# Queueing the negation of each prefetched projection tile behind an evacuation on ScalarE, in a hybrid decoder block

## The chip, the cores and the metric

The kernel runs on one core of one Trainium2 chip. The metric is the device time of one execution in microseconds (us), as the median over several runs. The engines that matter are TensorE (PE: matmuls into PSUM), VectorE (DVE), ScalarE (ACT), GpSimd (POOL) and SyncE (SP). Each engine works through its own instruction list in the order in which the program was laid out; semaphores tie the lists together. DMAs are issued from SP's list and from POOL's.

## The reference, cut to what matters

One decoder layer over a sequence of 512 tokens and a width of 1024, in float32: an RMS norm, one wide input projection `proj = h @ w_in`, cut into the parts `xr, gr, q, k, v, iq, ik, iw, g_a, g_b`; a recurrent branch (a causal convolution of `xr`, an RG-LRU scan, times `gelu(gr)`); a sparse attention branch, in which an indexer (`iq, ik, iw`) picks 128 keys for each query; then

```
merged = sigmoid(g_a) * y_a + sigmoid(g_b) * y_b
x = x + rms_norm(merged @ w_o)
x = x + rms_norm((silu(h @ w_ffn_gate) * (h @ w_ffn_up)) @ w_ffn_down)
```

The part at issue is `h @ w_in`.

## The kernel before

**Splitting.** Float32 precision is kept by splitting each operand into a rounded part `hi` and a rest `lo = x - hi`. One projection of 128 output columns (`mm3_steps`, L278) is then 24 matmuls of 128x512: for each of eight row blocks `hi*hi` (L281), `hi*lo` (L283), `lo*hi` (L285), all into one PSUM bank from `acc()` (L66), of which there are two that take turns.

**Units.** The weight tiles are numbered as *units* in the order in which they are used: u0 to u3 the indexer's queries, u4 to u11 the eight `gr` tiles, u12 to u27 pairs of `xr` tiles and pairs of `g_a` tiles in turn, u28 one `g_b` tile, u29 the first keys tile, u30 and u31 the first two queries tiles, u32 to u39 the RNN's output weights, u40 to u53 the other queries, keys and `g_b` tiles. Those of `w_in` except u0 and u1 are of kind "d" (44 of them): `do_load` (L204) issues a DMA on POOL (L220) that lands the tile rounded as `hi`. `do_split` (L240) then does two things: ACT writes `lo = -hi` (L243, the *negation*), and POOL issues a second DMA of the same tile that adds it to `lo` (L244, the *adding DMA*). The tiles live in six places: four named `ws`, and two pairs named `raw`. Every third unit uses a `raw` pair. A place is free again when PE is through with its unit.

**The order.** `take(u)` (L258) is called just before the matmuls of unit u. It loads up to u+5 and splits up to u+3. After the matmuls an ACT instruction evacuates the bank: `rope` (L474) for queries and keys, the gelu (L569) for `gr`, a copy into `xpad` (L577) for `xr`, a copy into `ma` (L626) for `g_a`, a copy into `gs` (L681) for `g_b`. A scheduler lays out each engine's list beforehand, by a simulated timeline: it may put a negation earlier on ACT than the program text does, when the simulation finds its data there and ACT free. On the chip an engine doesn't step past an instruction that waits.

**Around it.** In the gelu stage (about 60 to 127 us) PE also does the indexer's score matmuls; `lru_inputs` (L571) runs from `xpad` over `xc` (three DVE steps, L581) and its split `xcs` (L84) to the gate matmuls (L587, L588) and the sigmoids, and `lru_scan` (L600) goes on with exponentials, square roots and a scan. From u40 on the projections are threaded between the steps of attention, where PE's order is that of the program.

Of the kernel before, what the change touches and what calls it, by code (L numbers as in the profile page):

```python
# [11 lines left out]
AF = mybir.ActivationFunctionType  # L12
# [4 lines left out]
S = 512  # L17
# [28 lines left out]
def hybrid_block(ctx: ExitStack, tc: tile.TileContext, x, norm_mix_pre, w_in, conv_w, conv_b, rg_w_a,  # L46
# [4 lines left out]
    V, SC, G, PE = nc.vector, nc.scalar, nc.gpsimd, nc.tensor  # L51
# [14 lines left out]
    def acc():  # L66
        return psum.tile([P, 512], F32, name="acc", tag="acc")

    def ps_s():
        return ps_mix.tile([P, 512], F32, name="ps_s", tag="s", bufs=3)  # L70

    def ps_t():
        return ps_mix.tile([P, 512], F32, name="ps_t", tag="t", bufs=2)
# [4 lines left out]
    def f(ap):  # L78
        return ap.bitcast(F32)

    after = {}

    def split(src, hi, lo, lo_engine=None):
        return SC.copy(hi, src).ins, (lo_engine or V).tensor_tensor(lo, src, f(hi), op=A.subtract).ins  # L84
# [33 lines left out]
    def heap(shape, dt=F32R, name="hp"):  # L118
        return mixp.tile(shape, dt, name=name, tag="heap", bufs=14)
# [22 lines left out]
    for c in range(2):  # L142
        ps = ps_t()
# [96 lines left out]
    def do_split(u):  # L240
        if units[u][3] == "d":
            hi, lo = held.pop(u)
            SC.mul(lo, f(hi), -1.0)  # L243
            G.dma_start(lo, units[u][1], accum_op=A.add)  # L244
            wss[u] = [h.rearrange("p (k c) -> p k c", c=P) for h in (hi, lo)]
            return
        raw, ws = held.pop(u)
        with ExitStack() as order:
            for ins in after.pop(u + 2, ()) if u < 2 else ():
                order.enter_context(tc.issue_after(ins))  # L250
            split(raw, ws[:, 0], ws[:, 1])
        wss[u] = ws[:, 0], ws[:, 1]
# [5 lines left out]
    def take(u, ahead=3):  # L258
        load_ahead(u)
        while state["split"] <= min(u + ahead, state["load"] - 1):  # L260
            s = state["split"]
            if units[s][3] == "r" or s > u + 2 and units[s][3] == "s":
                break
            do_split(s)
            state["split"] += 1
        return wss.pop(u)
# [11 lines left out]
    def mm3_steps(ps, ws, hi, lo, order=None):  # L278
        order = order or list(range(KT))
        for n, k in enumerate(order):  # L280
            pe(PE.matmul(ps, ws[0][:, k, :], hi(k), start=(n == 0), stop=False))  # L281
            yield
            pe(PE.matmul(ps, ws[0][:, k, :], lo(k), start=False, stop=False))  # L283
            yield
            pe(PE.matmul(ps, ws[1][:, k, :], hi(k), start=False, stop=(n == len(order) - 1)))  # L285
            yield

    def mm3(*args, **kw):
        for _ in mm3_steps(*args, **kw):
            pass  # L290
# [88 lines left out]
    for t in range(NT):  # L379
        if t + 1 < NT:  # L380
            first_norm(t + 1)
        ps = acc()
        for k in range(KT):
            hi, lo = hT[:, 0, k, t * P:(t + 1) * P], hT[:, 1, k, t * P:(t + 1) * P]
# [48 lines left out]
    ps = ps_s()  # L433
# [3 lines left out]
    def col(n, m):  # L437
        return pcol[:, n * KT + m:n * KT + m + 1]
# [28 lines left out]
    ma = [map_.tile([P, S], F32, name=f"ma{m}") for m in range(KT)]  # L467
# [3 lines left out]
    def rope(ps, factor=1.0):  # L471
        xe = tmpp.tile([P, S], F32, name="rp_x", tag="t0")
        xs = tmpp.tile([P, S], F32, name="rp_s", tag="t1")
        SC.activation(xe, ps, AF.Copy, scale=factor)  # L474
        V.stream_shuffle(xs, xe, swap)
        G.tensor_tensor(xe, xe, rope_c, op=A.mult)
        G.tensor_tensor(xs, xs, rope_s, op=A.mult)
        V.tensor_tensor(xe, xe, xs, op=A.add)
        return xe
# [11 lines left out]
    for m in range(4):  # L491
        ps = acc()
        mm3(ps, take(u_iq[m]), h_hi, h_lo)
        iq.append(stack_q(rope(ps)))
# [53 lines left out]
    def load_gate_weights(m):  # L548
        raw = rnnp.tile([P, 2, P], F32, name="gw_raw", tag="gw_raw", bufs=2)
        ws = rnnp.tile([P, 2, 2, P], F32R, name="gw", tag="gw", bufs=2)  # L550
        G.memset(raw, 0.0)
        for n, w in enumerate((rg_w_a, rg_w_x)):
            ld(raw[0:HD, n, 0:HD], w[0, 2 * m])
            ld(raw[HD:P, n, HD:P], w[0, 2 * m + 1])
        split(raw, ws[:, 0], ws[:, 1], G)
        gw[m] = ws

    def shared(shape, tag, bufs):
        return rnnp.tile(shape, F32, name=tag, tag=tag, bufs=bufs)

    ys, gl, rr, tt, iu = [], {}, {}, {}, {}
    last = {}

    def gelu_gate(m):
        ps = acc()
        mm3(ps, take(u_gr[m]), h_hi, h_lo)
        if m % 2 == 0:
            gl[m] = heap([P, 2, S], F32, "gl")
        SC.activation(gl[m - m % 2][:, m % 2, :], ps, AF.Gelu_apprx_tanh)  # L569

    def lru_inputs(m):  # L571
        load_gate_weights(m)
        ps = acc()
        mm3(ps, take(u_xr[m]), h_hi, h_lo)
        xp = tmpp.tile([P, S + 3], F32, name="xpad", tag="t0")
        G.memset(xp[:, 0:3], 0.0)
        SC.copy(xp[:, 3:S + 3], ps)  # L577
        xc = tmpp.tile([P, S], F32, name="xc", tag="t1")
        SC.activation(xc, xp[:, 0:S], AF.Identity, bias=col(4, m), scale=col(0, m))
        for j in range(1, 4):  # L580
            V.scalar_tensor_tensor(xc, xp[:, j:j + S], col(j, m), xc, op0=A.mult, op1=A.add)  # L581
        xs = heap([P, 2, S], name="xcs")
        split(xc, xs[:, 0, :], xs[:, 1, :])
        gps = []
        for n in range(2):
            ps = ps_s()
            PE.matmul(ps, gw[m][:, 0, n, :], xs[:, 0, :], start=True, stop=False)  # L587
            PE.matmul(ps, gw[m][:, 0, n, :], xs[:, 1, :], start=False, stop=False)  # L588
            PE.matmul(ps, gw[m][:, 1, n, :], xs[:, 0, :], start=False, stop=True)
            gps.append(ps)  # L590
        rr[m], tt[m], iu[m] = shared([P, S], "rr", 4), shared([P, S], "tt", 4), shared([P, S], "iu", 4)
        SC.activation(rr[m], gps[0], AF.Sigmoid, bias=col(5, m))
        sig = SC.activation(iu[m], gps[1], AF.Sigmoid, bias=col(6, m))
        with tc.issue_after(sig.ins):
            last[m] = SC.activation(tt[m], rr[m], AF.Tanh, scale=sp4[:, m:m + 1])
        G.tensor_tensor(iu[m], iu[m], xc, op=A.mult)
# [26 lines left out]
    def gate_a(m):  # L623
        ps = acc()
        mm3(ps, take(u_ga[m]), h_hi, h_lo)
        SC.copy(ma[m], ps)  # L626

    for m in range(KT):
        gelu_gate(m)
        drain(3)  # L630
    for m in range(0, KT, 2):
        lru_inputs(m)
        lru_inputs(m + 1)
        if m > 0:
            lru_scan((m - 2, m - 1))
        gate_a(m)
        gate_a(m + 1)
        drain(2)
# [15 lines left out]
    def keys(m):  # L654
        ps = acc()
        yield from mm3_steps(ps, take(u_k[m]), h_hi, h_lo)
        r = rope(ps)
        for n in range(2):
            t = heap([P, 2, S], name="kst")
            src = r[n * HD:(n + 1) * HD]  # L660
            own = t[n * HD:(n + 1) * HD, 0, :]
            oth = t[(1 - n) * HD:(2 - n) * HD, 0, :]
            SC.copy(own, src)
            SC.copy(oth, src)
            V.tensor_tensor(t[0:HD, 1, :], src, f(own), op=A.subtract)
            V.tensor_tensor(t[HD:P, 1, :], src, f(own), op=A.subtract)
            ks[2 * m + n] = t


    def queries(m):  # L670
        ps = acc()
        yield from mm3_steps(ps, take(u_q[m]), h_hi, h_lo)
        qs[m] = stack_q(rope(ps, -(HD ** -0.5)))
# [3 lines left out]
    def gate_b(m):  # L677
        ps = acc()
        yield from mm3_steps(ps, take(u_gb[m]), h_hi, h_lo)
        gs = tmpp.tile([P, S], F32, name="gs", tag="t0")  # L680
        SC.copy(gs, ps)  # L681
        ld(gb_dram[m], gs)

    qs = {}
    for gen in [gate_b(m) for m in range(1)] + [keys(0), queries(0), queries(1)]:
        for _ in gen:
            pass
# [103 lines left out]
    for m in range(KT):  # L791
        ps = acc()
# [38 lines left out]
    def bank2():  # L831
        return psx.tile([P, 512], F32, name="bank2", tag="y", bufs=2)

    ps0 = [bank4() for _ in range(NT)]
    for n, k in enumerate(korder):
        if k % 2 == 0:
            ws = take(u_wo[0, k])
        for t in range(NT):
            hi, lo = mg[k][:, 0, t * P:(t + 1) * P], mg[k][:, 1, t * P:(t + 1) * P]
# [26 lines left out]
    for t in range(NT):  # L866
        ps1 = acc()
        for n, k in enumerate(korder):
            w = wo1[k]
            hi, lo = mg[k][:, 0, t * P:(t + 1) * P], mg[k][:, 1, t * P:(t + 1) * P]  # L870
# [16 lines left out]
        for half in range(2):  # L887
            ps = bank2()
# [286 lines left out]
```

## Time and profile before

| what | value |
|---|---|
| median of 3 runs | 927.35 us (925.54 to 927.96) |
| the profiled execution | 927.87 us, of which its span is 926.1 us |
| ACT busy | 497.4 us (54%) |
| DVE busy | 615.6 us (66%) |
| POOL busy | 229.3 us (25%) |
| mean granted clock of PE | 0.975 |
| TensorE clock in 40 slices, tenths | 9998998999989979999999998999999999999999 |

The times come from executions without the profiler; the rows come from the one profiled execution, and differences are made against its own time. Busy shares say how much an engine did, not what it waited for. A 9 in the row of the clock is full speed, 2.4 GHz; lower digits are slices in which the engine had half of that for a while.

### The profile page before, as it was taken

How to read it: one execution, taken by the hardware profiler on the slowest of the kernel's cores; microseconds unless marked ns; L12 is line 12 of the kernel's file. 1: busy time of each engine (PE TensorE's matmuls, PEld its weight loads, DVE VectorE, ACT ScalarE, POOL GpSimd, SP SyncE). 2: the span in 40 equal slices, each digit the busy share in tenths (PEclk: the TensorE clock that was granted, in tenths of full speed). 3: DMA queues.
4: the chain of work that ended last, by engine and by line, in shares of the span. 5: the costliest groups of instructions: out<-in, count | busy, mean ns of one | idle time of the engine just before them, and what ended most of it. 6: DMA issues, size and time to landing. Idle time of an engine off the chain costs nothing.

```text
span 926.1 us, 12988 instructions
## 1 busy us (share of the span) xinstructions
PE 873.5 (94%) x4811; PEld 750.6 (81%) x4811; DVE 615.6 (66%) x1109; ACT 497.4 (54%) x839; POOL 229.3 (25%) x242
## 2 busy tenths in 40 slices
PE   8989978989979979999999998999999999999996
PEld 5877756767668768888878887999999999988885
DVE  7675667885684148767756558978888887534415
ACT  6344336668733178777754346666666656333302
POOL 3362213355251143221012300323332332100000
PEclk9998998999989979999999999999999999999999
DMA  9667556657534654640454754687887788433203
GB/s 297 136 142 165 113 132 140 142 128 151 145 91 94 156 114 91 119 103 20 124 159 139 234 157 141 155 173 175 186 185 174 185 183 187 154 114 92 69 0 137
DMA packets 65698, 129.74 MB, mean 140 GB/s; under 512 B 8865, under 2 KB 32481, under 8 KB 65634
## 3 DMA queue, kind: packets, MB, share of 16 engines
q0 software_dynamic: 18432, 61.87, 33.3%
q1 hardware_dynamic: 46048, 64.92, 22.4%
q10 hardware_dynamic: 1154, 2.10, 0.6%
q8 instruction: 38, 0.62, 0.3%
q14 instruction: 26, 0.21, 0.1%
HBM read 122.59 MB, written 6.29 MB: 139 GB/s over the span
## 4 chain that ended last, share of the span: by engine, by line
PE 53%; issue 15%; DMA 14%; DVE 7%; ACT 5%; POOL 4%; SPq 0%; POOLq 0%; DVEq 0%; ACTq 0%
DMA ws<-in_t_ff_dram 6%; DMA ws<-in_t_in_dram 4%; PE acc L283 4%; PE acc L281 4%; PE acc L285 4%; PE bank L987 4%; PE bank L985 4%; PE bank L986 4%; PE bank L1060 3%; PE bank L1059 3%; PE bank L1061 3%; PE ps_o L739 2%; PE ps_t L729 2%; PE acc L1060 1%; PE acc L1059 1%
## 5 line engine op out<-in xcount | busy, mean ns | idle before, releaser
L281 PE MATMUL acc<-hT,ws 128*128 128x512 f32 x248 | 101.6, 410 | 8.9 <-ACT xpad L577 5.7
L84 DVE TENSOR_TENSOR ws<-raw,ws 128x1024 fp32r<-128x1024 f32 x44 | 61.2, 1394 | 66.0 <-ACT ws L84 65.8
L283 PE MATMUL acc<-hT,ws 128*128 128x512 f32 x248 | 100.8, 406 | 0.0
L285 PE MATMUL acc<-hT,ws 128*128 128x512 f32 x248 | 100.3, 404 | 0.0
L84 ACT CAST ws<-raw 128x1024 fp32r<-128x1024 f32 x44 | 46.1, 1052 | 70.6 <-PE bank L1061 37.6
L243 ACT ACTIVATE ws<-ws 128x1024 fp32r<-128x1024 f32 x29 | 30.7, 1059 | 88.0 <-DMA ws<-in_t_in_dram 83.0
L979 POOL DMA_DIRECT2D ws<-in_t_ff_dram x40 | 35.3, 883 | 153.7 <-ACT ws L978 80.9
L84 ACT CAST ws<-sums 128x1024 fp32r<-128x1024 f32 x40 | 40.1, 1048 | 50.9 <-DVE sums L969 50.0
L281 PEld LDWEIGHTS acc<-hT,ws 128*128 128x128 f32 x248 | 48.0, 194 | 21.3 <-ACT xpad L577 7.0
L987 PE MATMUL bank<-T,ws 128*128 128x256 f32 x200 | 57.6, 289 | 1.4 <-DMA ws<-in_t_ff_dram 0.8
L985 PE MATMUL bank<-T,ws 128*128 128x256 f32 x200 | 56.5, 283 | 0.4 <-ACT ws L84 0.4
L986 PE MATMUL bank<-T,ws 128*128 128x256 f32 x200 | 56.5, 282 | 0.0
L986 PE MATMUL bank<-B,ws 128*128 128x256 f32 x200 | 56.3, 282 | 0.0
L283 PEld LDWEIGHTS acc<-hT,ws 128*128 128x128 f32 x248 | 48.1, 194 | 10.1
L285 PEld LDWEIGHTS acc<-hT,ws 128*128 128x128 f32 x248 | 47.9, 193 | 10.2
L985 PE MATMUL bank<-B,ws 128*128 128x256 f32 x200 | 56.1, 281 | 0.0
L987 PE MATMUL bank<-B,ws 128*128 128x256 f32 x200 | 55.9, 280 | 0.0
L244 POOL DMA_DIRECT2D ws<-in_t_in_dram x29 | 25.7, 887 | 116.5 <-ACT ws L243 100.0
L281 PE MATMUL acc<-hT,raw 128*128 128x512 f32 x120 | 49.8, 415 | 4.0 <-ACT gl L569 4.0
L84 DVE TENSOR_TENSOR ws<-sums,ws 128x1024 fp32r<-128x1024 f32 x40 | 47.8, 1233 | 7.6 <-ACT ws L84 7.5
L283 PE MATMUL acc<-hT,raw 128*128 128x512 f32 x120 | 50.1, 417 | 0.0
L285 PE MATMUL acc<-hT,raw 128*128 128x512 f32 x120 | 49.6, 413 | 0.0
(330 smaller groups left out, 2716.1 us busy)
## 6 DMA issues: line engine op xcount, KB each, us to landing
ws<-in_t_in_dram POOLq DMA_DIRECT2D x58, 512.0 KB, 5.7
raw<-in_t_ff_dram SPq DMA_DIRECT2D x40, 512.0 KB, 4.5
raw<-in_t_in_dram POOLq DMA_DIRECT2D x30, 512.0 KB, 5.5
raw<-in_w_ffn_down_dram SPq DMA_DIRECT2D x22, 512.0 KB, 3.6
ws<-in_t_ff_dram POOLq DMA_DIRECT2D x20, 512.0 KB, 5.6
ws<-in_t_ff_dram POOLq DMA_DIRECT2D x20, 256.0 KB, 6.8
raw<-in_w_rnn_out_dram SPq DMA_DIRECT2D x8, 512.0 KB, 5.7
raw<-in_w_att_out_dram SPq DMA_DIRECT2D x8, 512.0 KB, 3.7
```

The costliest lines, as they stand in the source:

```text
L84: return SC.copy(hi, src).ins, (lo_engine or V).tensor_tensor(lo, src, f(hi), op=A.subtract).ins
L243: SC.mul(lo, f(hi), -1.0)
L281: pe(PE.matmul(ps, ws[0][:, k, :], hi(k), start=(n == 0), stop=False))
L283: pe(PE.matmul(ps, ws[0][:, k, :], lo(k), start=False, stop=False))
L285: pe(PE.matmul(ps, ws[1][:, k, :], hi(k), start=False, stop=(n == len(order) - 1)))
L979: G.dma_start(dst[:, 1], t_ff[n, m].rearrange("p (k c) -> p k c", c=P)[:, k], accum_op=A.add)
L985: PE.matmul(ps, a[:, 0, k, :], b[:, 0, k, :], start=(k == 0), stop=False)
L986: PE.matmul(ps, a[:, 0, k, :], b[:, 1, k, :], start=False, stop=False)
L987: PE.matmul(ps, a[:, 1, k, :], b[:, 0, k, :], start=False, stop=(k == 3))
L1059: PE.matmul(ps, a[:, 0, ts], b[:, 0, cs], start=(k == 0), stop=False)
L1060: PE.matmul(ps, a[:, 0, ts], b[:, 1, cs], start=False, stop=False)
L1061: PE.matmul(ps, a[:, 1, ts], b[:, 0, cs], start=False, stop=(k == FT - 1))
```

## The change

The negation's place on ACT gets a lower bound. Each of the five evacuations leaves its instruction in `after["evac"]`, and `do_split` lays the negation behind the last one left there, with an order on ACT's own list (`issue_after`). `take(u)` splits unit u+3 before the matmuls of u are laid out, so the last evacuation known is that of u-1: the negation of unit s now stands behind the evacuation of unit s-4. Units u2 and u3 are split before any evacuation is known and are as before. The RNN's output projections (u32 to u39) leave nothing in `after["evac"]`, so the negations of u40 to u43, split while they run or at the start of u40, stand behind that of u31 only.

```diff
     def do_split(u):
         if units[u][3] == "d":
             hi, lo = held.pop(u)
-            SC.mul(lo, f(hi), -1.0)
+            with ExitStack() as order:
+                if "evac" in after:
+                    order.enter_context(tc.issue_after(after["evac"]))
+                SC.mul(lo, f(hi), -1.0)
             G.dma_start(lo, units[u][1], accum_op=A.add)
...
     def rope(ps, factor=1.0):
-        SC.activation(xe, ps, AF.Copy, scale=factor)
+        after["evac"] = SC.activation(xe, ps, AF.Copy, scale=factor).ins
...
     def gelu_gate(m):
-        SC.activation(gl[m - m % 2][:, m % 2, :], ps, AF.Gelu_apprx_tanh)
+        after["evac"] = SC.activation(gl[m - m % 2][:, m % 2, :], ps, AF.Gelu_apprx_tanh).ins
...
     def lru_inputs(m):
-        SC.copy(xp[:, 3:S + 3], ps)
+        after["evac"] = SC.copy(xp[:, 3:S + 3], ps).ins
...
     def gate_a(m):
-        SC.copy(ma[m], ps)
+        after["evac"] = SC.copy(ma[m], ps).ins
...
     def gate_b(m):
-        SC.copy(gs, ps)
+        after["evac"] = SC.copy(gs, ps).ins
```

## Rows read from the trace of the kernel before

**Rows 1.** The page's busy time of each engine: us, share of span, instructions.
```profile
PE 873.5 (94%) x4811; PEld 750.6 (81%) x4811; DVE 615.6 (66%) x1109; ACT 497.4 (54%) x839; POOL 229.3 (25%) x242
```
**Rows 2.** Who waited for whom: us in total, times, longest us.
```profile
POOL ws L244 <- ACT ws L243: 100.0, 23, 7.7
ACT ws L243 <- DMA ws<-in_t_in_dram: 83.0, 23, 7.8
...
ACT raw L243 <- DMA raw<-in_t_in_dram: 26.1, 9, 6.3
...
POOL iu L614 <- ACT tt L611: 15.7, 4, 5.0
```
**Rows 3.** The same view for PE alone.
```profile
PE ps_s L587 <- ACT xcs L84: 6.5, 4, 3.8
PE acc L281 <- ACT xpad L577: 5.7, 3, 2.9
PE ps_t L729 <- DVE pt L84: 5.4, 4, 3.0
...
PE acc L281 <- ACT gl L569: 4.0, 1, 4.0
...
PE acc L281 <- ACT ma L626: 3.0, 1, 3.0
```
**Rows 4.** ACT in time, 128 to 139 us: start, us, instruction, [idle before <- releaser].
```profile
128.50 1.06 ACT L243 ACTIVATE ws<-ws 128x1024 fp32r<-128x1024 f32 x1 [4.98 <-DMA ws<-in_t_in_dram]
129.47 0.57 ACT L577 COPY xpad<-acc 128x512 f32<-128x512 f32 x1
...
137.20 1.06 ACT L243 ACTIVATE raw<-raw 128x1024 fp32r<-128x1024 f32 x1 [6.26 <-DMA raw<-in_t_in_dram]
138.16 0.60 ACT L84 CAST xcs<-xc 128x512 fp32r<-128x512 f32 x1
```
**Rows 5.** ACT in time, three places elsewhere.
```profile
154.22 1.06 ACT L243 ACTIVATE ws<-ws 128x1024 fp32r<-128x1024 f32 x1 [2.57 <-DMA ws<-in_t_in_dram]
...
190.35 1.06 ACT L243 ACTIVATE ws<-ws 128x1024 fp32r<-128x1024 f32 x1 [2.70 <-DMA ws<-in_t_in_dram]
...
335.39 1.06 ACT L243 ACTIVATE ws<-ws 128x1024 fp32r<-128x1024 f32 x1 [5.09 <-issue]
```
**Rows 6.** ACT in time, 58 to 71 us.
```profile
58.89 1.06 ACT L243 ACTIVATE ws<-ws 128x1024 fp32r<-128x1024 f32 x1 [3.89 <-DMA ws<-in_t_in_dram]
...
60.15 0.59 ACT L474 ACTIVATE rp_x<-acc 128x512 f32<-128x512 f32 x1
...
70.61 0.60 ACT L569 ACTIVATE gl<-acc 128x512 f32<-128x512 f32 x1
```
**Rows 7.** PE in stretches of 8 us: busy time (instructions), granted clock, DMA share, GB/s.
```profile
71.26:79.26 8.00, 8.00 (x24) 0.63 0.74 191
...
138.82:146.82 8.00, 7.27 (x24) 0.80 0.61 131
159.90:167.90 8.00, 8.00 (x23) 0.63 0.44 118
196.65:204.65 8.00, 8.00 (x28) 0.79 0.32 81
```
**Rows 8.** PE in time: the first matmuls of units u0 and u1.
```profile
31.19 0.40 PE L281 MATMUL acc<-hT,ws 128*128 128x512 f32 x1
...
36.77 0.39 PE L281 MATMUL acc<-hT,ws 128*128 128x512 f32 x1
```
**Rows 9.** The view of line L244, its last line: from issue to landing.
```profile
DMA to landing us min/median/max: 5.4/5.6/8.8
```
**Rows 10.** POOL in time, 95 to 97 us.
```profile
95.71 0.87 POOL L244 DMA_DIRECT2D ws<-in_t_in_dram  x1 [6.84 <-ACT ws L243]
96.28 0.86 POOL L220 DMA_DIRECT2D ws<-in_t_in_dram  x1
```
**Rows 11.** ACT in time, the negation that waited for the load of rows 10.
```profile
103.36 1.06 ACT L243 ACTIVATE ws<-ws 128x1024 fp32r<-128x1024 f32 x1 [5.85 <-DMA ws<-in_t_in_dram]
```

## The prediction, written before the changed kernel ran

> **What bounds the kernel now.** I read the page first: PE is busy 873.5 us of 926.1, so at most 52.6 us of the span are PE's idle time, and every other engine is far from full [rows 1]. What can be won is PE idle time, and the slow clock that follows it. The list of all waits shows something odd on ACT: the largest waits of this half-idle engine are those of the negation for the DMA of its own tile, 83.0 us in 23 waits and 26.1 us in 9 more, and POOL sits 100.0 us behind the same negations [rows 2]. ACT does nothing else in those 109.1 us, because its list is worked in order. Whether that matters is read from PE's own waits: its long ones end with ACT's evacuations and casts, which shared a list with those negations: `xpad` 5.7 us, `xcs` 6.5, `gl` 4.0, `ma` 3.0; and one of 3.0 that ends with DVE's part of `pt`, itself behind ACT's cast [rows 3].
>
> ACT in time shows the mechanism. At 128.50 a negation starts after 4.98 us of waiting for its DMA, and `xpad`, the evacuation that PE's next projection needs, follows at 129.47; at 137.20 the next one starts after 6.26 us, and `xcs`, for which the gate matmuls wait, follows at 138.16 [rows 4]. Counting negations in unit order (every third goes to a `raw` place), the first is u17's and the second u18's, while `xpad` here is the evacuation of u12. So the list has the negation five units ahead of the evacuation that it holds up, and its tile isn't needed before PE has worked off five projections.
>
> **The change, part by part.** It adds and removes no instruction and no DMA; an order within one engine's list needs no wait of its own. So the direct cost is nil; 44 negations of 1.06 us [rows 4] stay 46.6 us on ACT, at other places.
>
> *What moves.* Unit s's negation goes behind the evacuation of s-4: u17's behind that of u13, that is past `xpad` of u12; u18's, behind u14's, past `xcs`. The same holds at the negations of 154.22 (u20, ahead of the `ma` copy), 190.35 (u25, ahead of an `xpad`), 335.39 (u46, ahead of a `pt` cast) [rows 5] and 58.89 (u8, ahead of the rope evacuation of u3 at 60.15, from which the query stacking runs that the gelu evacuation of 70.61 stood behind) [rows 6]. Not moved are u2, u3, and u40 to u43, so PE's wait for a softmax tile near 322 us, behind u43's negation, stays.
>
> *The stalls that go.* A stall goes if the negation's wait and its 1.06 us exceed it. Near 130 and 138 they do, 4.98 and 6.26 against an `xpad` wait below 2.9 and an `xcs` wait of 3.8 [rows 3, 4]. At 154.22 and 190.35 it is 2.57 + 1.06 = 3.63 and 2.70 + 1.06 = 3.76 against 3.0 (`ma`) and 2.9 (`xpad`): enough by under 1 us. At 335.39 it is 5.09 + 1.06 against 3.0, but a DVE step stands between. At 58.89 it is 3.89 + 1.06 = 4.95 against 4.0, through a chain over POOL and DVE [rows 3, 5, 6].
>
> *The clock.* After a stall PE runs for some us at the lower of its two levels, 1.2 instead of 2.4 GHz: in the 8 us from 71.26, the end of the `gl` stall, the mean granted clock is 0.63, so 0.37 x 8 = 2.96 us are lost; the same after `ma` at 159.90, and (a third such stretch, not shown) after 337.46. After `xcs` at 138.82 it is 0.20 x 8 = 1.60, after `xpad` at 196.65 0.21 x 8 = 1.68 [rows 7].
>
> *The sum.* Two groups:
> - Sure in mechanism: `xpad` 5.7 - 2.9 = 2.8, `xcs` 6.5, its clock 1.6: 10.9 us, in full.
> - Thin margin or a chain through another engine: `xpad` 2.9 + 1.68, `gl` 4.0 + 2.96, `ma` 3.0 + 2.96, `pt` 3.0 + 2.96: 23.5 us, of which I take half, 11.7.
>
> That is 22.6 us; all of it would be 34.4.
>
> *What is late next.* Three things may take some back. First the adding DMA, now issued later: behind the waiting negation on ACT are casts and sigmoids, and behind the adding DMA, on POOL, the loads of later tiles, the rope products and the scan's products; who waits for those is PE, by way of DVE. There are two banks, so PE can't start unit s-2 before the evacuation of s-4, and from there to the start of s lie two projections, 2 x (36.77 - 31.19) = 11.2 us [rows 8]. Negation (1.06) and landing (5.6 median, 8.8 at most) take 6.7 to 9.9 us [rows 4, 9]: it fits, with 1.3 to 4.5 us to spare. Second the load: POOL issues it when PE has freed its place, six units back, and the negation comes after the evacuation two units later, 11.2 us on, against 7.08 us that a load took from its issue at 96.28 to the negation at 103.36 [rows 10, 11]; so that wait mostly ends, and only a new neighbour on ACT pays 1.06 us. Third the recomputed lists: every engine's order shifts a little. For a stall that the trace before doesn't show I can give only bounds: nothing, or the case below. I take one of the size of the second `xpad` stall, 2.9 + 1.68 = 4.6 us.
>
> So 22.6 - 4.6 = 18.0 us come off the profiled execution's 927.87, giving 909.9. That execution lies 0.5 us above the median of 927.35, so the prediction is 909.4, rounded to **909 us**.
>
> One rule speaks against the change. The Trainium skill, "DMA: Bandwidth & Descriptors", section "Queues, rings and completion order", says that each DMA engine takes the descriptors of a ring in ring order. By it, an adding DMA issued right behind a load lands later than one with the ring to itself; the trace agrees, for the load right behind an adding DMA took up to 7.08 us where adding DMAs take 5.6 in the median [rows 9 to 11]. With the load ahead, by this rule, the spare time would be 11.2 - 1.06 - 7.08 = 3.1 us rather than 4.5: enough still, but it is part of the slow rival.
>
> **The rivals.**
> - *All of it* (0.12): no new stall, 927.9 - 34.4 - 0.5 = 893. For it: the negations' 109.1 us [rows 2] are more than three times what is asked of them. Against: some of it hangs on margins below 1 us.
> - *Only the first places* (0.17): the `ma`, later `xpad`, `gl` and `pt` stalls are kept by the table loads, the DVE steps and the casts around them, and only 10.9 us come, less 4.6: 927.9 - 6.3 - 0.5 = 921. For it: those margins.
> - *The wait only changes its name* (0.10): PE's stalls come back under other releasers, or the scheduler puts other waiting work ahead of the evacuations: 927. This is also the case in which the change doesn't do what it says. Against: ACT's busy time is 54% [rows 1], and the loads get 11.2 us.
> - *The adding DMA comes too late* (0.18), slower. Place: the recurrent stage, u16 to u31. A negation held by a neighbour on ACT, or an adding DMA held on POOL behind a scan product (longest wait 5.0 us [rows 2]) and behind a load, takes 1.06 + 7.08 + 5.0 = 13.1 us against 11.2 [rows 8, 10, 11], and PE stops at its third matmul. Priced at 4.6 us a stall as above, four late tiles of the 16 eat the 18.0; at seven, 7 x 4.6 - 18.0 = 14.2 come on top: 941. Against: it takes two delays at once, and a late PE gives the DMA more time.
>
> **How the numbers follow.** The forecast has 0.43, the rivals 0.12, 0.17, 0.10 and 0.18. A difference counts from 0.3%, 2.8 us: faster is below 924.6, slower above 930.1. The forecast and the first two rivals are faster: 0.72; same 0.10; slower 0.18. The range goes from 892 to 931: it leaves out nearly all of the slow rival, and little below.
>
> **What would show it.** Right: in the list of waits the negation's wait for its DMA falls from 109.1 us below 30; ACT in time shows evacuations starting within 1 us of the last matmul in the gelu stage; PE's waits for `xpad`, `xcs`, `gl` and `ma` shrink from 19.2 us (the four rows) to below 8, and the clock's low slices between 60 and 210 us go. POOL's wait for the negation need not fall, since the negation itself is later. Wrong: PE waiting at L285 for a DMA of `ws` or `raw` (the late adding DMA), or the same stalls with table loads or DVE as releasers. Two numbers would break the reasoning: negations that still wait long for loads, or stalls that go without the time going with them.

## The result, and the profile after

The changed kernel takes 890.57 us (median of 4, 889.10 to 891.81) beside 927.38 for the kernel before on the same chip: ratio 0.9606, 95% interval 0.9586 to 0.9626. It is faster by 36.8 us, twice the 18.0 that I forecast. The profiled execution took 890.67 us with a span of 888.8, against 927.87 and 926.1 before.

The page, busy time and the slices of PE's granted clock:

```profile
PE 857.5 (96%) x4811; PEld 740.9 (83%) x4811; DVE 620.6 (70%) x1109; ACT 494.7 (56%) x838; POOL 229.2 (26%) x242
...
PEclk9999999999899999999999999999999999999998
```

PE's busy time fell from 873.5 [rows 1] to 857.5: the same 4811 instructions took 16.0 us less, and the mean granted clock rose from 0.975 to 0.991. PE's idle time (span less busy) fell from 52.6 to 31.3, 21.3 us. The two make up the 37.3 us of the span. The clock's stretches of [rows 7] no longer have their dips; the same windows of the changed kernel (it is elsewhere in its work by then) show PE at the higher of its two levels, 2.4 GHz, throughout (two of the four):

```profile
71.26:79.26 8.00, 8.00 (x38) 1.00 0.99 214
138.82:146.82 8.00, 8.00 (x36) 1.00 0.91 170
```

All waits, the lines that answer to [rows 2]:

```profile
POOL ws L220 <- PE acc L288: 64.4, 14, 11.8
...
POOL ws L247 <- ACT ws L246: 41.8, 14, 7.7
ACT ws L246 <- DMA ws<-in_t_in_dram: 23.2, 3, 8.8
...
POOL raw L247 <- ACT raw L246: 18.4, 7, 6.0
```

The negation's wait for its own DMA fell from 109.1 us in 32 waits to 23.2 in 3, and those three are u40, u42 and u43. The line on top is the one to notice: POOL now issues loads (L220) as soon as **PE** has freed a place, and not as soon as ACT has let it past an adding DMA. PE's own waits, which answer to [rows 3]:

```profile
PE acc L284 <- ACT rp_x L477: 4.1, 1, 4.1
PE ps_t L732 <- DVE pt L84: 2.4, 4, 1.0
...
PE acc L284 <- ACT xpad L580: 1.4, 1, 1.4
...
PE acc L284 <- ACT gl L572: 1.2, 1, 1.2
...
PE ps_t L732 <- ACT sm L717: 0.8, 1, 0.8
```

`xpad`, `gl`, `xcs` (0.2) and `ma` (none) were 19.2 us and are 2.8. Only `rp_x`, u30's rope evacuation behind the casts of the keys, is still near its old size (5.2 before). ACT in the gelu stage:

```profile
93.97 0.60 ACT L572 ACTIVATE gl<-acc 128x512 f32<-128x512 f32 x1 [3.46 <-PE acc L288]
94.47 1.05 ACT L246 ACTIVATE ws<-ws 128x1024 fp32r<-128x1024 f32 x1
...
100.84 0.60 ACT L572 ACTIVATE gl<-acc 128x512 f32<-128x512 f32 x1 [3.60 <-PE acc L288]
101.33 1.05 ACT L246 ACTIVATE ws<-ws 128x1024 fp32r<-128x1024 f32 x1
```

Evacuations now wait for PE, which is what they should wait for; the negation follows at once, its tile long there. In the kernel before it was the negation that waited, 5.85 us at 103.36 [rows 11], with an evacuation behind it.

**Where the time came from.** Two stretches before, and two after with the same number of PE instructions (length, PE busy, PEld, DVE, ACT, POOL, granted clock, DMA share, GB/s):

```profile
94.00:160.00 66.00, 54.81 (x224) 42.02 (x222) 44.96 (x110) 29.05 (x45) 16.86 (x26) 0.97 0.56 119
160.00:236.00 76.00, 71.26 (x282) 55.50 (x282) 60.12 (x98) 52.83 (x75) 33.22 (x40) 0.94 0.68 150
```

```profile
94.00:160.00 66.00, 66.00 (x285) 53.25 (x284) 61.06 (x132) 39.24 (x58) 24.31 (x35) 1.00 0.80 164
160.00:215.00 55.00, 51.94 (x221) 40.91 (x220) 46.52 (x69) 45.53 (x68) 28.00 (x31) 1.00 0.74 152
```

506 PE instructions took 142 us before and 121 us after. The lead of the changed kernel (its start of a unit against the same start before) says the same: 7.0 us at u13, 22.9 at u18, 27.8 at u31, 29.3 at u40, 38.9 at u42, and 37.6 from u54 to the end.

**The theory that I then tested: a closed loop set the pace.** Where it holds, the kernel before works like this: POOL issues the load of a tile right behind the adding DMA of the tile before it [rows 10]; the negation on ACT waits for that load [rows 11]; the adding DMA on POOL waits for the negation [rows 2]; and behind it stands the next load. So one tile takes a turn of load, negation and issue, and since each evacuation stands behind one negation in ACT's list, PE can in the long run take a projection per turn and no faster. The negations ahead of and behind that of [rows 11] show the turn in the gelu stage:

```profile
94.35 1.06 ACT L243 ACTIVATE ws<-ws 128x1024 fp32r<-128x1024 f32 x1 [5.25 <-DMA ws<-in_t_in_dram]
...
111.83 1.06 ACT L243 ACTIVATE raw<-raw 128x1024 fp32r<-128x1024 f32 x1 [5.20 <-DMA raw<-in_t_in_dram]
```

With 103.36 between them that is 9.0 and 8.5 us a tile, where a projection alone takes PE about 5.6 us [rows 8] and a unit of this stage, which has score matmuls beside it, about 7.0. PE isn't held there at once. From 94 to 112 us it was busy all the time (18.0 us of 18, granted clock 1.00), and the longer turn only used up the lead that the negations had over PE: u13's began as PE began u9, u18's while PE was still in u14. From u13 on it shows. PE's starts of u13, u18 and u31, before and after:

```profile
121.61 0.50 PE L281 MATMUL acc<-hT,ws 128*128 128x512 f32 x1
...
168.28 0.39 PE L281 MATMUL acc<-hT,raw 128*128 128x512 f32 x1
...
258.08 0.40 PE L281 MATMUL acc<-hT,ws 128*128 128x512 f32 x1
```

```profile
114.60 0.39 PE L284 MATMUL acc<-hT,ws 128*128 128x512 f32 x1
...
145.34 0.39 PE L284 MATMUL acc<-hT,raw 128*128 128x512 f32 x1
...
230.31 0.39 PE L284 MATMUL acc<-hT,ws 128*128 128x512 f32 x1
```

The five units from u13 to u18 took 46.7 us before and 30.7 after, the thirteen from u18 to u31 89.8 and 85.0. So of the 20.8 us gained here, 15.9 came in five units. In the other thirteen the loop mostly didn't set the pace: of their negations in the kernel before, four had no wait at all and only one waited over 4 us.

The change opens the loop: the negation waits for PE by way of the evacuation, its load was issued about two units earlier, and so in these tiles neither ACT nor POOL waits for a DMA. It doesn't open it everywhere. The negations of u40, u42 and u43, which stand behind u31's evacuation only, still follow one another by 8.3 us (274.56, 282.86, 291.10) and wait for their loads each time; PE loses 0.8 us there.

In the expectations below, D is this loop.

### The profile page after: what moved, and what is told of

Same layout as the page of the kernel before. It is cut to its first block, busy times and chain, and to the rows that moved or that the text cites. A ratio compares the mean times of both kernels' runs of the same rounds, so it can differ in the third digit from the quotient of the medians.

```text
span 888.8 us, 12985 instructions
## 1 busy us (share of the span) xinstructions
PE 857.5 (96%) x4811; PEld 740.9 (83%) x4811; DVE 620.6 (70%) x1109; ACT 494.7 (56%) x838; POOL 229.2 (26%) x242
## 4 chain that ended last, share of the span: by engine, by line
PE 62%; DVE 13%; DMA 8%; issue 8%; ACT 7%; POOL 2%; SPq 0%; DVEq 0%; ACTq 0%; POOLq 0%
PE acc L286 6%; PE acc L284 6%; PE acc L288 6%; PE bank L990 5%; DMA ws<-in_t_ff_dram 5%; PE bank L988 4%; PE bank L989 4%; PE bank L1064 3%; PE bank L1062 3%; PE bank L1063 3%; PE ps_o L742 2%; PE ps_t L732 2%; DVE xc L584 2%; PE acc L990 1%; PE acc L988 1%
## 5 line engine op out<-in xcount | busy, mean ns | idle before, releaser
L284 PE MATMUL acc<-hT,ws 128*128 128x512 f32 x248 | 98.7, 398 | 1.4 <-ACT xpad L580 1.4
L286 PE MATMUL acc<-hT,ws 128*128 128x512 f32 x248 | 99.0, 399 | 0.0
L288 PE MATMUL acc<-hT,ws 128*128 128x512 f32 x248 | 98.7, 398 | 0.0
L84 ACT CAST ws<-sums 128x1024 fp32r<-128x1024 f32 x40 | 40.1, 1048 | 52.6 <-DVE sums L972 51.7
L284 PEld LDWEIGHTS acc<-hT,ws 128*128 128x128 f32 x248 | 46.7, 188 | 11.8 <-ACT xpad L580 1.9
L286 PEld LDWEIGHTS acc<-hT,ws 128*128 128x128 f32 x248 | 46.7, 188 | 10.0
L288 PEld LDWEIGHTS acc<-hT,ws 128*128 128x128 f32 x248 | 46.7, 188 | 9.8
L284 PE MATMUL acc<-hT,raw 128*128 128x512 f32 x120 | 48.0, 400 | 1.2 <-ACT gl L572 1.2
L286 PE MATMUL acc<-hT,raw 128*128 128x512 f32 x120 | 48.1, 401 | 0.0
L288 PE MATMUL acc<-hT,raw 128*128 128x512 f32 x120 | 47.7, 398 | 0.0
L246 ACT ACTIVATE ws<-ws 128x1024 fp32r<-128x1024 f32 x29 | 30.7, 1059 | 23.2 <-DMA ws<-in_t_in_dram 23.2
L973 POOL TENSOR_TENSOR sums<-raw 128x512 f32<-128x512 f32 x20 | 33.5, 1675 | 34.7 <-PE acc L990 10.8
```

The costliest lines, as they stand in the source:

```text
L973: G.tensor_tensor(s3, a11, a21, op=A.subtract)
```

## Experiments

**One stage at a time.** Three kernels, each the kernel before with the new `do_split` and only the evacuations named leaving their instruction in `after["evac"]`.

The gelu stage alone:

```diff
-        SC.activation(gl[m - m % 2][:, m % 2, :], ps, AF.Gelu_apprx_tanh)
+        after["evac"] = SC.activation(gl[m - m % 2][:, m % 2, :], ps, AF.Gelu_apprx_tanh).ins
```

> Only the gelu evacuations leave their instruction for the negations to queue behind; the negations of u8 to u16 move, all others stand as in the kernel before. Theory A (each stall on PE that a waiting negation causes on ACT goes with that negation, and nothing else changes): the gl stall and its slow clock go, which in the full change had moved unit u7 forward by 6.1 us; the xpad, xcs, ma and later stalls stay. 4 to 7 us faster than before: 920 to 923 us. Theory B (the gain comes from all engine lists having been laid out anew, whichever negations move): no fixed share, 890 to 927 us, with the later stalls changed as well.

Measured: 923.46 us, ratio 0.9922 (0.9895 to 0.9949). The total came out near what was expected, but by luck, since the `gl` stall did not go (`PE acc L284 <- ACT gl L572: 3.3, 1, 3.3`). The profiled execution was the fastest of the seven, 918.67 us. Its lead was 12.0 us at u18 and then, in the unmoved recurrent stage, went back to 4.4 at u27, as three `xpad` waits of 8.8 us came up. It was 11.5 again at u32, where the kernel before waits 5.2 us for u30's rope evacuation and this one 2.2 at most. So a lead read at one unit alone can mislead.

The recurrent stage alone:

```diff
-        SC.copy(xp[:, 3:S + 3], ps)
+        after["evac"] = SC.copy(xp[:, 3:S + 3], ps).ins
...
-        SC.copy(ma[m], ps)
+        after["evac"] = SC.copy(ma[m], ps).ins
```

> Only the evacuations into xpad and into ma leave their instruction; the negations of u16 to u31 move. Theory A: what the full change won between units u13 and u23 comes alone, 27.8 - 7.0 = 20.8 us, 904 to 909 us; the gl stall of 4.0 us and the stalls of attention stay. Theory B: no fixed share. Theory C (my halving was right, and the late stalls of ma and xpad went by luck of the new lists): 10.9 + half of 9.2 = 15 us, 912 us.

Measured: 908.16 us, 0.9773 (0.9753 to 0.9792). PE's waits:

```profile
PE ps_t L732 <- DVE pt L84: 7.2, 5, 3.8
PE acc L284 <- ACT gl L572: 4.1, 1, 4.1
PE acc L284 <- ACT rp_x L477: 4.1, 1, 4.1
PE ps_t L732 <- ACT sm L717: 4.0, 1, 4.0
```

`gl` and `sm`, which belong to other stages, are there; `xcs` and `ma` have gone from the top. The lead grew to 21.6 us at u33 and stayed above 20 to the end.

The attention's part alone, u44 and on, by `gate_b` and, once the recurrent stage's first gate weights are there (`gw`), by `rope`:

```diff
-        SC.activation(xe, ps, AF.Copy, scale=factor)
+        ins = SC.activation(xe, ps, AF.Copy, scale=factor).ins
+        if gw:
+            after["evac"] = ins
...
-        SC.copy(gs, ps)
+        after["evac"] = SC.copy(gs, ps).ins
```

> Only the rope evacuations of keys and queries after the recurrent stage and those of g_b leave their instruction; the negations of u44 and later move, all before stand as they did. Theory A: the full change moved unit u42 forward by 9.6 us more than unit u40 and lost 1.3 us of it after; so 7 to 9 us faster, 918 to 921 us, and the stall that ends with the first softmax tiles (3.4 us before) shrinks below 1.5 us although u43's negation stands where it did, because the adding DMA of u44 no longer runs beside u40's load. Theory C (my reading: that stall is not touched): only the stall of pt goes, 3 to 6 us, 921 to 925 us, softmax stall still 3 us or more.

Measured: 921.88 us, 0.9916 (0.9891 to 0.9941). PE's wait for `sm` fell from 3.4 us to 1.5, and the lead rose from -1.2 at u40 to 7.8 at u42. Of that lead 6.3 us were there at the end. The three parts together, 0.78 + 2.27 + 0.84 = 3.89%, and with the indexer's part below, 0.16, 4.05%, agree with the change's 3.94% within the intervals: whole stages add up.

**Single places.** First the order on the indexer's rope evacuations alone, which moves only the first negations (u4 to u8):

```diff
-        SC.activation(xe, ps, AF.Copy, scale=factor)
+        ins = SC.activation(xe, ps, AF.Copy, scale=factor).ins
+        if not gw:
+            after["evac"] = ins
```

> Only the rope evacuations of the indexer's queries leave their instruction; the negations of u4 to u8 move, u8's only past the rope evacuation of u3. Theory A, if the gl stall hangs on the chain from that rope evacuation over POOL and DVE to the query stacking: 3 to 6 us faster, 921 to 924 us. If it hangs on a negation between the stacking and the gelu: no change, 926 to 929 us. Theory B: no fixed share.

Measured: 927.65 us, 0.9984 (0.9970 to 0.9999). The `gl` stall did fall, to under 1 us, and the lead was 5.7 us at u7 and u8. Then it went: 4.9 at u9, 3.1, 1.1, and -0.5 at u12, given back in waits of which the kernel before has only 0.6 us:

```profile
PE ps_s L513 <- ACT relu L516: 5.0, 6, 1.9
```

This is where the loop can be seen to hold PE. PE starts u10 and u11, and ACT negates u14 and u15:

```profile
97.74 0.40 PE L284 MATMUL acc<-hT,ws 128*128 128x512 f32 x1
...
106.67 0.40 PE L284 MATMUL acc<-hT,ws 128*128 128x512 f32 x1
```

```profile
102.78 1.06 ACT L246 ACTIVATE ws<-ws 128x1024 fp32r<-128x1024 f32 x1 [5.66 <-DMA ws<-in_t_in_dram]
...
112.21 1.06 ACT L246 ACTIVATE raw<-raw 128x1024 fp32r<-128x1024 f32 x1 [6.16 <-DMA raw<-in_t_in_dram]
```

The negations from u12 to u15 follow one another by 8.6, 8.8 and 9.4 us, and POOL issues each load right behind the adding DMA (95.93 behind 95.38, 104.75 behind 104.21) without having to wait for PE. PE, which is earlier here by the `gl` stall, needs 8.7, 8.9 and 9.8 us for u9 to u11, with waits for relus that ACT does behind the negations. In the kernel before it needed 6.9, 7.0 and 8.2 for them.

Then two negations in the middle of the loop, those ahead of the `ma` and the later `xpad` stall [rows 5]:

```diff
-                if "evac" in after:
+                if "evac" in after and u in (20, 25):
```

> The kernel before with only two negations queued behind their evacuations: u20's, ahead of the ma copy, and u25's, ahead of the second xpad. These are the two of my thin-margin group in the recurrent stage. Full credit for them is 3.0 + 2.96 + 2.9 + 1.68 = 10.6 us: 917 to 920 us. Half, as I took it: 922 to 924 us. If the gain of single places is given back to the chain of loads and negations in front of the next tiles: 926 to 930 us.

Measured: 927.68 us, 0.9991 (0.9976 to 1.0007), nothing, where the full price of the two stalls with their slow clock was 10.5 us:

```profile
PE ps_s L590 <- ACT xcs L84: 11.3, 8, 4.0
PE ps_t L732 <- ACT sm L717: 6.4, 1, 6.4
```

The `ma` and `xpad` waits shrank, `xcs` rose from 6.5 to 11.3, and the lead of 5.9 us at u23 was -1.0 at u25. It came back to 5.6 at u33 and was lost again by u42, partly to the longer `sm` wait. This and the run before it are what counting stalls one by one can't give, and what a pace set elsewhere does give. Both also recompute every list, and a new order that brings stalls of its own isn't ruled out here.

**Opening the loop from the other side.** The kernel before, its evacuations still behind its negations on ACT; on POOL the adding DMA of a tile goes behind the load of the next:

```diff
-                G.dma_start(hi, w)
+                loads[l] = G.dma_start(hi, w).ins
...
-            G.dma_start(lo, units[u][1], accum_op=A.add)
+            with ExitStack() as order:
+                if u + 1 in loads:
+                    order.enter_context(tc.issue_after(loads[u + 1]))
+                G.dma_start(lo, units[u][1], accum_op=A.add)
```

> The kernel before, with ACT's order left alone; only on POOL the adding DMA of unit s is queued behind the load of s+1, so that this load no longer stands behind an adding DMA that waits for a negation. Theory D (load, negation, adding DMA and next load close a loop through the two lists; its turn of 8.2 to 9.0 us sets the pace of the tiles, because each evacuation stands behind a negation): the loop now spans two tiles, so it no longer sets the pace, and most of the 36.8 us come without touching ACT: 892 to 908 us, with a negation's wait for its DMA well below 109 us. Theory A (what counts is that no negation stands ahead of an evacuation on ACT): negations still stand there, and wait nearly as long for loads that now share the ring with the adding DMA behind them: 915 to 930 us.

Measured: 906.89 us, 0.9756 (0.9728 to 0.9783), without any order on the evacuations. POOL issues both DMAs back to back, every 6.4 to 7.1 us, and what it waits for is PE:

```profile
94.38 0.55 POOL L220 DMA_DIRECT2D ws<-in_t_in_dram  x1 [5.04 <-PE acc L288]
94.95 0.88 POOL L247 DMA_DIRECT2D ws<-in_t_in_dram  x1
100.79 0.55 POOL L220 DMA_DIRECT2D raw<-in_t_in_dram  x1 [4.96 <-PE acc L288]
101.36 0.89 POOL L247 DMA_DIRECT2D ws<-in_t_in_dram  x1
...
107.87 0.57 POOL L220 DMA_DIRECT2D ws<-in_t_in_dram  x1 [5.12 <-PE acc L288]
```

ACT still waits for the loads, though less, 68.6 us instead of 109.1:

```profile
ACT ws L243 <- DMA ws<-in_t_in_dram: 52.5, 22, 7.9
...
ACT raw L243 <- DMA raw<-in_t_in_dram: 16.1, 10, 3.0
```

So opening the loop on POOL alone brings 21.5 of the 36.8 us. Up to the end of these projections it brings more: PE starts the first product with the attention's output (`ot`) at 449.26 instead of 476.01, a lead of 26.8 us, and 5.2 of that are lost in the feed-forward part, which the edit doesn't name but whose lists are new too (PE waits 2.9 us there for a cast of weights, 0.4 before). What the order on ACT adds isn't measured alone; the `gl` stall, which is still 4.8 us here, is one place for it.

**The negation twice.** An extra 1.06 us a tile should cost its full sum where the loop sets the pace, and little where it is open.

```diff
-                SC.mul(lo, f(hi), -1.0)
+                for _ in range(2):
+                    SC.mul(lo, f(hi), -1.0)
```

On the changed kernel:

> The changed kernel with each negation written twice on ACT. Theory D: the loop is open, the second negation costs only ACT's time, of which 44% is free: 890 to 897 us. If ACT's busy time or the later adding DMA sets the pace in the changed kernel: 905 us or more, as much added as in the kernel before.

Measured: 895.95 us, 0.9641 (0.9618 to 0.9663) of the kernel before. ACT is busy 534.4 us instead of 494.7, and the time rose by 5.4 by the medians, or 3.2 by the two ratios, each taken against the kernel before on its own chip: with the loop open this work is nearly free. On the kernel before:

> The kernel before with each negation written twice on ACT (44 more instructions of 1.06 us). Theory D: the loop's turn grows by 1.0 to 1.1 us a tile, and where it sets the pace (some 20 to 27 tiles from u5 to u31, a few after u40) the time grows with it: 945 to 958 us. Theory A (single stalls): each of the seven stalls on PE grows by up to 1 us with some slow clock: 932 to 940 us.

Measured: 921.10 us, 0.9917 (0.9885 to 0.9950), faster, against every theory here. The lists, recomputed with the higher cost, are others: in the gelu stage negations come in pairs (87.17 and 91.32, 100.53 and 104.79), the first of a pair waits for its DMA and the second doesn't, and POOL issues two loads in a turn:

```profile
93.77 0.90 POOL L245 DMA_DIRECT2D ws<-in_t_in_dram  x1 [3.16 <-ACT ws L244]
94.34 0.89 POOL L220 DMA_DIRECT2D ws<-in_t_in_dram  x1
97.50 0.55 POOL L220 DMA_DIRECT2D raw<-in_t_in_dram  x1 [2.27 <-PE acc L286]
```

The negation's wait for its DMA fell to 69.9 us. So this run changed the order as well as the cost, and it tells D neither right nor wrong. A doubled cost tests a kernel with a list scheduler only if the lists stay.

**The negation on POOL.** The kernel before with the negation taken off ACT's list altogether:

```diff
-            SC.mul(lo, f(hi), -1.0)
+            G.tensor_scalar(lo, f(hi), -1.0, None, op0=A.mult)
```

> The kernel before, with each negation written by POOL instead of ACT (44 instructions of 128x1024 on POOL, no ordering edge). ACT can then hold up no evacuation, but POOL still does load, negation, adding DMA and next load one after the other, as in the kernel before, where tile followed tile at 8.2 to 9.0 us in the gelu stage. Theory A (ACT's list held up by a waiting negation is all of it): the ACT stalls go, 900 to 915 us, less what POOL's slower negation costs. Theory D (the chain of load, negation, adding DMA, next load sets a pace, and the change wins by breaking it: loads no longer stand behind a negation that waits): no gain or slower, 925 to 960 us, with PE waiting for DMAs of ws and raw or for the rope products behind them on POOL.

Measured: 924.50 us, 0.9975 (0.9956 to 0.9994). The evacuations were free of it and the lead was 16.6 us at u18, but one negation takes POOL 2.8 to 3.7 us, 2.96 in the mean:

```profile
100.21 3.17 POOL L243 TENSOR_SCALAR ws<-ws 128x1024 fp32r<-128x1024 f32 x1
```

In the recurrent stage, where POOL also has the scan's products, all of the lead was lost (-7.3 at u31; waits of 8.0 us for `xcs`, 7.4 for `ma`), of which u30's rope evacuation, now not waited for, gave back 8 by u33. Inconclusive: the gelu stage fits either theory, and the recurrent stage measures POOL.

**How far behind.** The changed kernel with the negation behind the evacuation of s-5 (all five evacuations as here):

```diff
-        after["evac"] = SC.copy(ma[m], ps).ins
+        after["prev"], after["evac"] = after.get("evac"), SC.copy(ma[m], ps).ins
...
-                if "evac" in after:
-                    order.enter_context(tc.issue_after(after["evac"]))
+                if after.get("prev"):
+                    order.enter_context(tc.issue_after(after["prev"]))
```

> The changed kernel, but the negation of unit s is queued behind the evacuation of s-5, one projection earlier than s-4. That is just past the evacuation that it held up before. Its load, issued when PE is through with s-6 and landing 4 to 7 us later, is then not always there, so the negation waits up to 2 us, in front of casts and sigmoids but no longer of the evacuation. Theory A: most of the gain stays, 893 to 905 us, with a negation's wait for its DMA of 30 to 70 us in all (109 before, 23 after). If the place behind s-4 is what counts and one earlier falls back to the old order: 915 to 928 us.

Measured: 895.45 us, 0.9648 (0.9607 to 0.9689). The load has one projection less (5.6 us by [rows 8]) until the negation asks for it; the negation's wait for its DMA is 39.2 us in 9 waits (30.4 in 7 for `ws`, 8.8 in 2 for `raw`) instead of 23.2 in 3, and the `sm` stall is 3.4 us again.

Split two units ahead instead of three, so behind s-3:

```diff
-def take(u, ahead=3):
+def take(u, ahead=2):
```

> The changed kernel, but take(u) splits only up to u+2, so the negation of unit s is queued behind the evacuation of s-3. This tests the rival that I priced as slow: with two banks only one projection (5.6 us) and the first two matmuls lie between that evacuation and the first use of lo, against 1.06 us of negation and 5.6 us or more for the adding DMA to land. If that slack is what bounds the choice: PE waits for a DMA of ws or raw at the third matmul by 1 to 4 us in most of some 40 tiles where no other work lies between, and the time is 905 to 960 us, 925 as my figure, clearly above the 890.6 of the change. If the slack is never used up, it stays at 888 to 894 us.

Measured: 890.76 us, 0.9599 (0.9566 to 0.9632), the same as the change. With 5.6 us less between evacuation and use, the adding DMA was late twice in the whole run, by little; the second time at 205.65 by 0.56:

```profile
76.26 0.50 PE L288 MATMUL acc<-hT,ws 128*128 128x512 f32 x1 [0.66 <-DMA ws<-in_t_in_dram]
```

**The largest stall left.** The changed kernel with u30's rope evacuation ahead of the casts of the keys (`rope` cut into its evacuation and the rest, and the keys' rest ordered behind u30's evacuation):

```diff
-    for gen in [gate_b(m) for m in range(1)] + [keys(0), queries(0), queries(1)]:
...
+    mm3(ps, take(u_k[0]), h_hi, h_lo)
+    xk = rope_evac(ps)
+    ps = acc()
+    mm3(ps, take(u_q[0]), h_hi, h_lo)
+    xq = rope_evac(ps, -(HD ** -0.5))
+    with tc.issue_after(after["evac"]):
+        for _ in keys(0, xk):
+            pass
```

> The changed kernel, with one more ordering: the casts of the first keys are queued on ACT behind the rope evacuation of u30, for which PE waits 4.05 us at the first matmul of the RNN's output projection (unit u32) in the changed kernel. If that wait is only ACT's order: it falls below 1.5 us, and with the slow clock behind it 4 to 6 us go: 884 to 887 us. If the stall comes back a unit later, as PE's waits for u31's evacuation and for DVE's product, as in the two kernels with the negation one place earlier or later: 888 to 891 us.

Measured: 892.93 us, 0.9606 (0.9578 to 0.9633), no gain over the change, whose ratio is the same. The stall of 4.1 went and the lead at u33 was 34.0, but by u35 it was 30.0 against the change's 29.3, and new waits stand in the list:

```profile
PE acc L284 <- ACT rp_x L479: 1.9, 2, 1.0
PE acc L284 <- DVE ma L658: 1.9, 1, 1.9
```

**The softmax stall.** My prediction said that PE's wait near 322 us, behind u43's negation, stays; it fell from 3.4 us to 0.8. In the kernel before, u44's adding DMA (299.03) stands right ahead of u40's load (299.77) on POOL; the change takes it away from there. Here it alone is taken away:

```diff
-                if "evac" in after:
+                if "evac" in after and u in (44,):
```

> The kernel before, with the order for the negation of u44 alone, so that its adding DMA leaves POOL and the ring in front of u40's load. Ring theory (the softmax stall near 322 us came from that adding DMA): the negation of u40 waits for its load less than before, 3.9 us from the load's issue instead of 6.0, and PE's wait for sm falls from 3.4 us to 1.0 to 1.8. Rival (the stall went in the changed kernel because of all that came before it): the wait for sm stays at 3 to 4 us. Time: by the theory of the pace one stall less is given back or nearly so, 924 to 929; if single stalls counted in full, 3.4 and its clock less, 922 to 923.

Measured: 926.77 us, 0.9984 (0.9966 to 1.0003). POOL and then ACT:

```profile
300.82 0.54 POOL L220 DMA_DIRECT2D ws<-in_t_in_dram  x1 [4.55 <-PE acc L288]
```

```profile
304.80 1.06 ACT L246 ACTIVATE ws<-ws 128x1024 fp32r<-128x1024 f32 x1 [8.76 <-DMA ws<-in_t_in_dram]
```

Load to negation is 3.98 us instead of 305.73 - 299.77 = 5.96, and PE waits 1.33 us instead of 3.37:

```profile
324.89 0.33 PE L732 MATMUL ps_t<-ident,sm 128*128 128x128 f32 x1 [1.33 <-ACT sm L717]
```

That is what the ring theory expected; two DMAs that merely share the engines would look the same, and no run tells the two apart. The lead rose from -1.0 us at u40 to 1.9 at u42 and was 1.3 at the end, so 2.3 of the 2.9 us stayed in this trace: here the single stall was not given back. The median's difference is within what the runs can tell.

## Why the prediction was wrong

**What failed was the sum: the half, and the 4.6 us put against it.** The mechanism was right as far as it went, though it didn't see the loop. Of the four things named ahead, all came: the negation's wait fell below 30 us (23.2), evacuations follow PE's last matmul, the four PE waits went from 19.2 to 2.8, the clock's dips went. By the terms on record, all stalls in full are 34.4 us, 22.2 of PE's idle time and 12.2 of clock; the trace after shows 21.3 and 16.0. The sum went wrong in three steps:

1. *"Thin margin or a chain through another engine: ... 23.5 us, of which I take half."* I asked of each stall whether the wait of the one negation ahead of it exceeds it by enough. That question doesn't settle a stall's worth, since the stall is where the loop's lag shows and not where it arises. It fails in both directions: with exactly the negations of the `ma` and later `xpad` stall moved, nothing came (927.68), and with the first negations alone, where the `gl` stall went as it should, nothing came either (927.65). With a whole stage moved its worth came in full: 21 us for the recurrent stage alone, where by the margins I had put 10.9 as sure and the rest in doubt. The 11.7 us that I took off were there. A single stall can be worth its size all the same where no loop holds the stage behind it: with u44's negation alone moved, 2.0 us of the `sm` wait went and 2.3 us of lead stayed.
2. *A new stall of 4.6 us.* It didn't come. What is left at the old places is 1.2 us for `gl` and 1.4 for `xpad`, both where an evacuation stands behind other work on ACT. The spare time that I had worked out for the adding DMA, 1.3 to 4.5 us, was too small: a kernel with 5.6 us less of it had 0.66 + 0.56 us of late tiles. My slow rival has no ground here. What I set beside it, that an adding DMA lands later behind a load, does show. From issue to landing the adding DMAs took 5.6 us in the median before, 6.3 in the changed kernel, where they go out mostly one to two us behind a load, and 7.6 in the run that issues the load first, where they go out right behind it. The spare time took that. (The 7.08 us that I put in for it were a load's, up to the start of its negation.)
3. *"PE's wait for a softmax tile near 322 us, behind u43's negation, stays."* I followed the moved negations on ACT and not their adding DMAs in the ring, though I had the row that shows what a DMA ahead does. It fell by 2.5 us, and the clock behind it (0.79 in the 8 us from 326.35 before, 1.00 in those from 294.20 after) gives 0.21 x 8 = 1.7. The run with u44 alone shows that this DMA was the cause of 2.0 us of it. The Trainium skill, "DMA: Bandwidth & Descriptors", section "Queues, rings and completion order", says that each DMA engine consumes descriptors in ring order; what that costs a load behind an adding DMA it doesn't say. The runs fit it, 3.98 us against 5.96, without showing that order rather than sharing is the reason.

Put together: 18.0 + 11.7 + 4.6 + 4.2 = 38.5, against 37.3 of span measured. The rival "all of it", 893, was the right one, and my ground against it ("margins below 1 us") was the mistake. That it came within 3 us is partly luck: it left out the 4.2 us of the softmax stall and counted 2.8 us of stalls that are still there.

One reading was wrong without a part in the sum: near 130 us the tile of u17's negation was three projections off and not five, since PE had then finished u13.

**What is shown and what isn't.** That the loop through POOL held the kernel back is shown by the run that opens it on POOL alone (906.89), and in the gelu stage by the run with the indexer's part alone, where PE's units take as long as the loop's turn. That a single stall in these stages need not be worth its size is shown by the two runs that took some out; that the loop and not the new lists took the time back is shown for the indexer's part and not for the two negations. That an open loop makes ACT's extra work cheap is shown by the doubled negation on the changed kernel (3.2 to 5.4 us for 40). How the 36.8 us divide into the loop and the order on ACT is not: opening it on POOL gives 21.5, but both recompute the lists, as does every run here. Why doubling the negation made the kernel before faster is read from its lists (two tiles a turn) and was not tried apart from them.

## What to carry to other kernels

When one engine waits long and often for the DMA of a prefetched tile, don't price the bottleneck's stalls one at a time: follow the wait around (load, operation on it, the DMA issued behind that, the next load) and see whether it closes; if it does, compare its turn with the bottleneck's own time per tile. The difference times the tiles is an upper estimate of what opening it brings: the first tiles are covered by the lead that the prefetch has, and later ones count only where the loop still sets the pace (15.9 us in five units here, 4.8 in the next thirteen). Keep work on a prefetched tile behind what the bottleneck waits for now, and a load ahead of work that waits. A removed stall counts only if the stage behind it is not paced by something else.

## What the runs showed of the hardware

- The load of u40 took 5.96 us from issue to the operation that waits for it when it went right behind an adding DMA, and 3.98 with none right ahead of it (3.93 in the changed kernel).
- The same negation of a 128x1024 f32 tile takes 1.06 us on ACT and 2.96 in the mean on POOL (2.8 to 3.7).
- Here the granted clock made idle time cost a second time: 21.3 us less idle time on PE came with 16.0 us less busy time for the same 4811 instructions.
